# A hybrid encoder block: x2 read back behind the last sum's split, and the plain features' activations scaled by VectorE and made later

## The chip, the cores and the metric

The kernel runs on one core of one Trainium2 chip, as one program. The metric is the device time of an execution in microseconds (us). The time of the kernel before is the median of three runs, 719.93 us (717.46, 719.93 and 720.59).

## The reference

One layer of a streaming encoder on x of 512 tokens by 1024 channels, everything in float32. A first half (gated linear attention beside forgetting attention, merged by gates) gives the residual stream x2. The change lies in the second half, the gated MLP with a causal convolution of width 3 on its activation branch, and the final norm:

```python
    x = x + y @ w_out

    a, val = jnp.split(rmsnorm(x, norm_ffn_g) @ w_up, 2, axis=-1)
    a = causal_dwconv(a, conv_w, conv_b)
    return x + (jax.nn.gelu(a) * val) @ w_down
...
    return rmsnorm(x, norm_final_g)
```

`w_up` has 2 x 2816 columns (22 tiles of 128 features in each half), `w_down` 2816 rows.

## The kernel before, in words

**Splits.** Every product of matrices is made of three matmuls on halves in a reduced format (`mm3`, L248 to L250): high times high, low times high, high times low. So each piece of weights (128 x 1024 values) is loaded, cast by ScalarE to its high half (L217) and subtracted by VectorE to its low half (L218), into one of three pairs of buffers (`wh`, `wl`). `piece()` hands the pieces out in one fixed order and splits up to three ahead; a piece's buffers come free when TensorE is through with it.

**The up projection.** The first two feature tiles (`plain`) are made by plain products into four PSUM banks, for each tile one bank of activations `pa` and one of values `pv`. The other 20 tiles come in ten groups of two, by a scheme for 2 x 2 blocks with seven products instead of eight. Each group g has seven steps (g, p) with p from 1 to 7, and the steps of neighbouring groups are interleaved by a table (`SLOT`). A step is 24 matmuls of 256 columns. The operands of the seven products on the side of x are blocks of the normalised x2, or sums of them, kept as high and low halves (`xops`, made by `split_x`, L974 to L979). The tile `xo` holds those of products 1, 5 and 3. The weights of products 6, 7 and 4 are sums: the raw piece of an earlier step stays in its buffer, and when it has been split, a DMA on POOL's queue adds the next block to it in place (L225, `rawx<-in_wu_dram`). For a group that chain is 5 to 6 to 4, so the last sum of all is that of step (9, 4).

After step 6 and step 7 of a group, VectorE writes the activations before the convolution to the tile `ap` (L982, called from L1135 and L1137); `convolve` makes three taps (ScalarE at L1030, VectorE at L1034 twice) and the GELU (ScalarE, L1039) in the tile `t0`, of which there is one. After step 4, VectorE multiplies by the values (L1149) and makes sums for the down projection (`sums_of_acts`), which is done by seven products too. Its first pieces are multiplied already within the last group (`first_down`, after steps (9, 6) and (9, 7)).

**The plain features.** `plain_activations` (L1055) is called ahead of the fourth step (number 3 in the list of steps). For each of the two tiles: VectorE scales `pa` by the token's norm factor `rb` into `ap` (L1007 and L1059), `convolve` follows, POOL multiplies the GELU by `rb` in place (L1061), and VectorE multiplies that by `pv` from PSUM (L1062). At its end stand the sums and the first split of the two features (L1046, L1025, L1026). The table `ahead_of` (L1070) says what is called ahead of which step.

**x2's way back.** The first half writes x2 token by token to DRAM (`x2d`). It is read back into the place of `xo`, once the last product on `xo` is done, by a DMA on POOL's queue (L1162, 2 MB), together with the gain of the final norm, broadcast to all partitions (L1163). The first to read it are the additions of the down projection's products (`add`, L1227).

**Order.** Each engine runs its instructions in one fixed order, and DMAs are issued in the order of the queue of the engine that issues them (SyncE, POOL, ScalarE). The order is not simply that of the source: a planner runs the program dry with its own costs, takes among the instructions that are ready the one that is traced first or due first, and keeps that order. `tc.issue_after(i)` adds an edge, so that an instruction stands behind `i` on its engine.

Of the kernel before, what the change touches and what calls it, by code (L numbers as in the profile page):

```python
# [9 lines left out]
F32 = mybir.dt.float32  # L10
# [4 lines left out]
ALU = mybir.AluOpType  # L15
# [3 lines left out]
P = 128  # L19
T = 512  # L20
NT = T // P
D = 1024
# [28 lines left out]
NCL = 2  # L51
NSS = (NF - NCL) // 2
# [14 lines left out]
def hybrid_kernel(ctx: ExitStack, tc, xT, wp, wu, wd, wf, pp, aw2, qkg, fing, out):  # L67
    nc = tc.nc
# [33 lines left out]
    wsum = [dpool.tile([P, KB * 512], F32, name=f"wsum{i}") for i in range(4)]  # L102
# [19 lines left out]
    at_step = {}  # L122
# [50 lines left out]
    raws, splits, taken, first_copy, added, last_load = {}, [], [0], [], [], []  # L173
# [25 lines left out]
    def split_next():  # L199
        n = len(splits)  # L200
        if n not in raws:
            load_raw(n)
        raw, m = raws[n], recipes[n][2]
        if n in spare:
            hi, lo = spare[n]()
        else:
            hi = wpool.tile([P, 1024], F32R, tag="wh", name="wh", bufs=NW)
            lo = wpool.tile([P, 1024], F32R, tag="wl", name="wl", bufs=NW)
        if n < KD:
            if n > 0:  # L210
                nc.scalar.copy(out=hi[:, :WF], in_=raw)
            else:
                first_copy.append(nc.vector.tensor_copy(out=hi[:, :WF], in_=raw))  # L213
            nc.vector.tensor_sub(out=lo[:, :512], in0=raw[:, :512], in1=hi[:, :512].bitcast(F32))  # L214
            nc.vector.tensor_sub(out=hi[:, WF : WF + 64], in0=raw[:, 512:WF], in1=hi[:, 512:WF].bitcast(F32))
        else:
            nc.scalar.copy(out=hi[:, :m], in_=raw[:, :m])  # L217
            nc.vector.tensor_sub(out=lo[:, :m], in0=raw[:, :m], in1=hi[:, :m].bitcast(F32))  # L218
        splits.append((hi, lo))
        for what, i, *other in then.get(n, ()):  # L220
            if what == "load":
                load_raw(i)
            elif what == "add":
                raws[i] = raw
                added[:] = [nc.gpsimd.dma_start(raw, recipes[i][0], accum_op=ALU.add)]  # L225
            else:
                first_sum(i, *other, after=added[0])
        for i, b, c in sums_at.get(n, ()):
            if n < ADD_AT[0]:
                continue  # L230
            now = nc.gpsimd.tensor_copy(out=tick, in_=lo[:, 0:1].bitcast(F32))
            with tc.issue_after(now.ins):
                nc.gpsimd.dma_start(wsum[i][:, c], b[:, c], accum_op=ALU.add)

    def piece():
        n = taken[0]
# [70 lines left out]
    tick = cpool.tile([P, 1], F32, name="tick")  # L307
# [6 lines left out]
    def col(c, rows=P):  # L314
# [6 lines left out]
        out=negm, in_=negm, pattern=[[-1, P]], base=0, channel_multiplier=1, compare_op=ALU.is_ge, fill=-1e30  # L321
# [5 lines left out]
        out=gmask, in_=gmask, pattern=[[1, P]], base=0, channel_multiplier=-1, compare_op=ALU.is_ge, fill=0.0  # L327
# [5 lines left out]
    rb = cpool.tile([P, T], F32, name="rb")  # L333
# [79 lines left out]
    for k in range(KD):  # L413
        nc.scalar.activation(out=xh[k], in_=xrs[k], func=AF.Copy, scale=col(C_MIX + k))  # L414
        split_next()
        with tc.issue_after(first_copy[0].ins):
            nc.vector.scalar_tensor_tensor(
                out=xl[k], in0=xrs[k], scalar=col(C_MIX + k), in1=xh[k].bitcast(F32),
# [60 lines left out]
    for j in range(2):  # L479
# [4 lines left out]
            out=mz[:, j, :], in0=pz, scalar1=col(C_AB + j), scalar2=0.0, op0=ALU.add, op1=ALU.min  # L484
# [456 lines left out]
    for g in range(2):  # L941
        n = at_step[g, 5]
# [31 lines left out]
    def split_x(p, src, after=None):  # L974
        with tc.issue_after(after[0].ins) if after else ExitStack():
            hi = nc.scalar.copy(out=xops[p][0], in_=src)
        with tc.issue_after(after[1].ins) if after else ExitStack():
            lo = nc.vector.tensor_sub(out=xops[p][1], in0=src, in1=xops[p][0].bitcast(F32))
        return hi, lo  # L979
# [61 lines left out]
    def halves(x):  # L1041
        return x.rearrange("p (i t) -> p i t", t=H)

    def sums_of_acts(j, k):
        if j == 0:
            nc.vector.tensor_sub(out=s3[:, k], in0=a11[:, k], in1=a21[:, k])  # L1046
            split_act(0, a11, k)
        else:
            nc.vector.tensor_sub(out=s1[:, k], in0=a22[:, k], in1=a21[:, k])
            minus_sum(s2[:, k], s1[:, k], a11[:, k])  # L1050
            minus_sum(s4[:, k], a12[:, k], s2[:, k])

    last_gelu = None

    def plain_activations():  # L1055
        t0 = npool.tile([P, 2, T], F32, tag="t0", name="t0")
        for f, (pa, pv) in enumerate(plain):
            if f > 0:
                nc.vector.tensor_mul(out=ap[:, f, 2 : T + 2], in0=pa, in1=rb)  # L1059
            convolve(f, f, t0)  # L1060
            nc.gpsimd.tensor_mul(out=t0[:, f], in0=t0[:, f], in1=rb)  # L1061
            nc.vector.tensor_mul(out=act[0][:, :, f], in0=halves(pv), in1=halves(t0[:, f]))  # L1062
        sums_of_acts(0, slice(0, NCL))

    def p7_operand():
        nc.vector.tensor_sub(out=y3, in0=x11, in1=x21)
# [1 line left out]


    ahead_of = {  # L1070
        1: lambda: split_x(2, x12, third), 2: lambda: split_x(6, y2, third), 3: plain_activations, 4: p7_operand,
        5: lambda: split_x(4, x22, third),
    }

    def up_product(ps, p, first):
# [41 lines left out]

    st_of = {}
    for n, (g, p) in enumerate(steps):
        if n in ahead_of:  # L1120
            ahead_of[n]()
        st = st_of.setdefault(g, {})
        f = NCL + 2 * g
        name = {1: "x", 2: "x", 5: "z", 3: "z", 6: "y", 7: "y", 4: "y"}[p]
        first = name not in st
        if first:

            st[name] = (pax if name == "x" or g == 0 and name == "y" else pmm)()
        ps = st[name]
        up_product(ps, p, first)  # L1130
        if p in (1, 5, 3):
            st[p] = joint(ps)
        elif p == 6:
            nc.vector.tensor_add(out=ps, in0=ps, in1=st[1])
            minus_sum(ap[:, :, 2 : H + 2], halves(ps), halves(st[3]))  # L1135
        elif p == 7:
            minus_sum(ap[:, :, H + 2 : T + 2], halves(ps), halves(st[5]))  # L1137
            t0 = st["t0"] = npool.tile([P, 2, T], F32, tag="t0", name="t0")
            for i in range(2):
                convolve(f + i, i, t0)  # L1140
        elif p == 4:
            t0 = st["t0"]
            if f // KB == (f + 1) // KB:
                parts = [(f // KB, slice(f % KB, f % KB + 2), slice(0, 2))]
            else:
                parts = [((f + i) // KB, slice((f + i) % KB, (f + i) % KB + 1), slice(i, i + 1)) for i in range(2)]
            for i, c in enumerate((st["x"], ps)):
                for j, k, fs in parts:
                    nc.vector.tensor_mul(  # L1149
                        out=act[j][:, i, k], in0=halves(c)[:, fs], in1=t0[:, fs, i * H : (i + 1) * H]  # L1150
                    )
            for j, k, _ in parts:
                sums_of_acts(j, k)
        if g == NSS - 1 and p in EARLY:
            first_down(EARLY.index(p))
# [3 lines left out]
    xo2 = npool.tile([P, 6 * KH * H], F32, tag="xo", name="xo2")  # L1159
    x2t = xo2[:, : NT * D].rearrange("p (t d) -> p t d", d=D)  # L1160
    fgt = xo2[:, NT * D : (NT + 1) * D]
    nc.gpsimd.dma_start(x2t, x2d)  # L1162
    nc.gpsimd.dma_start(fgt, fing.broadcast_to([P, D]))  # L1163


    def in_place_of(tag, size):
# [210 lines left out]
```

## Time and profile before

| | us |
|---|---|
| median of three runs | 719.93 |
| profiled execution, its time | 717.68 |
| profiled execution, its span | 716.0 |
| TensorE busy | 703.1 (98%) |
| VectorE busy | 535.7 (75%) |
| ScalarE busy | 406.9 (57%) |
| POOL busy | 214.4 (30%) |
| mean granted clock of TensorE | 0.997 |

The profile is of one execution. Its span runs from the first to the last instruction; the execution's own time is 1.7 us longer. PE is TensorE, DVE VectorE, ACT ScalarE, POOL GpSimd, SP SyncE. A row of a timeline has start and duration in us, engine, line, operation, output and inputs, shape and count; in brackets stands how long the engine sat idle before it, and what ended that. A row of waits has who waited for whom, the us in total, the times, and the longest. The line of an operation is often that of a helper, such as `mm3`. [...] A row "DMA to landing" gives least, median and greatest time from issue to landing for the loads of one line.

The plain products end at 398.2 us, the steps run from there to 609.8 us, and the down projection to the end.

### The profile page before, as it was taken

Reading aid. Unit: us, or ns where it says so; the run is one execution under the profiler, and the core shown is the slowest. Engines: PE = TensorE matmul, PEld = TensorE weight load, DVE = VectorE, ACT = ScalarE, POOL = GpSimd, SP = SyncE. Lnnn points to the kernel's source line nnn. Section 1 sums busy time; section 2 is a strip of 40 time slices with the busy share of each in tenths; the row PEclk is TensorE's granted clock in tenths of the full one; section 3 lists DMA queues with packets and bytes.
Section 4 is the critical chain, followed back from the end, with each engine's and each line's share of the span. In section 5 each row is a group of like instructions: output and inputs, shape, how many; then the busy total and the mean of one; then the engine's idle time right before and its main releaser. Section 6 shows DMA issues by size and latency. Waiting matters only on the chain.

```text
span 716.0 us, 11179 instructions
## 1 busy us (share of the span) xinstructions
PE 703.1 (98%) x4186; PEld 612.9 (86%) x4186; DVE 535.7 (75%) x781; ACT 406.9 (57%) x646; POOL 214.4 (30%) x246
## 2 busy tenths in 40 slices
PE   8999999999999999999999999999999999999996
PEld 5887788888888888888788989999999998888885
DVE  7874596677866675566447988889888888997894
ACT  6484324588877742234553755565566565655663
POOL 7204333336342412223221252243434310000122
PEclk9999999999999999999999999999999999999998
DMA  8367745667568576766528488777777888576643
GB/s 282 123 237 199 257 142 198 221 153 181 152 135 202 120 194 159 171 166 163 176 89 253 115 177 191 171 180 180 184 174 192 203 188 298 165 220 202 178 147 118
DMA packets 45654, 129.87 MB, mean 181 GB/s; under 512 B 5000, under 2 KB 12312, under 8 KB 45472
## 3 DMA queue, kind: packets, MB, share of 16 engines
q1 hardware_dynamic: 31008, 92.91, 38.8%
q0 software_dynamic: 8352, 30.94, 24.9%
q10 hardware_dynamic: 6240, 5.31, 2.3%
q8 instruction: 33, 0.54, 0.3%
q14 instruction: 21, 0.17, 0.1%
HBM read 124.93 MB, written 27.28 MB: 213 GB/s over the span
## 4 chain that ended last, share of the span: by engine, by line
PE 87%; DVE 6%; ACT 3%; DMA 2%; issue 1%; SPq 0%; DVEq 0%; ACTq 0%
PE ps_mm L248 21%; PE ps_mm L249 21%; PE ps_mm L250 21%; PE ps_ax L250 6%; PE ps_ax L248 6%; PE ps_ax L249 6%; DVE wl L218 2%; DMA rawx<-in_wu_dram 1%; PE ps_pt L786 1%; ACT wh L217 1%; PE ps_po L810 1%; PE ps_ax L927 1%; DMA qf<-in_wf_dram 1%; DVE xs L1000 1%; PE ps_lg L760 1%
## 5 line engine op out<-in xcount | busy, mean ns | idle before, releaser
L248 PE MATMUL ps_mm<-xh,wh 128*128 128x512 f32 (+1 forms) x312 | 107.3, 345 | 1.0 <-DVE wh L213 1.0
L250 PE MATMUL ps_mm<-xh,wl 128*128 128x512 f32 (+1 forms) x312 | 106.5, 342 | 0.0
L249 PE MATMUL ps_mm<-xl,wh 128*128 128x512 f32 (+1 forms) x312 | 106.2, 341 | 0.0
L217 ACT CAST wh<-rawx 128x1024 fp32r<-128x1024 f32 x75 | 76.2, 1015 | 52.3 <-PE ps_mm L249 22.6
L218 DVE TENSOR_TENSOR wl<-rawx,wh 128x1024 fp32r<-128x1024 f32 x75 | 88.7, 1190 | 16.6 <-ACT wh L217 16.5
L217 ACT CAST wh<-raw 128x1024 fp32r<-128x1024 f32 x61 | 63.9, 1049 | 56.7 <-PE ps_mm L249 41.8
L218 DVE TENSOR_TENSOR wl<-raw,wh 128x1024 fp32r<-128x1024 f32 x61 | 84.0, 1377 | 10.4 <-ACT wh L217 7.4
L248 PEld LDWEIGHTS ps_mm<-xh,wh 128*128 128x128 f32 x312 | 59.1, 190 | 7.8 <-ACT xh L414 1.9
L250 PEld LDWEIGHTS ps_mm<-xh,wl 128*128 128x128 f32 x312 | 59.1, 190 | 7.6 <-DVE wl L214 0.5
L217 ACT CAST wh<-rawz 128x1024 fp32r<-128x1024 f32 x28 | 29.3, 1047 | 61.9 <-PE ps_mm L249 29.8
L249 PEld LDWEIGHTS ps_mm<-xl,wh 128*128 128x128 f32 x312 | 59.3, 190 | 5.9
L225 POOL DMA_DIRECT2D rawx<-in_wu_dram x30 | 26.1, 869 | 102.3 <-DVE wl L218 94.9
L248 PE MATMUL ps_mm<-wh,xh 128*128 128x512 f32 x140 | 55.4, 397 | 0.1
L249 PE MATMUL ps_mm<-wl,xh 128*128 128x512 f32 x140 | 54.7, 391 | 0.0
L250 PE MATMUL ps_mm<-wh,xl 128*128 128x512 f32 x140 | 54.6, 390 | 0.0
L218 DVE TENSOR_TENSOR wl<-rawz,wh 128x1024 fp32r<-128x1024 f32 x28 | 40.2, 1435 | 8.2 <-ACT wh L217 8.1
L191 POOL TENSOR_TENSOR rawx<-rawx,raw 128x256 f32<-128x256 f32 x32 | 38.2, 1222 | 25.4 <-DMA rawx<-in_wu_dram 25.4
L248 PE MATMUL ps_mm<-xo,wh 128*128 128x256 f32 x160 | 45.4, 284 | 0.0
L250 PE MATMUL ps_mm<-xo,wl 128*128 128x256 f32 x160 | 45.3, 283 | 0.0
L249 PE MATMUL ps_mm<-xo,wh 128*128 128x256 f32 x160 | 45.3, 283 | 0.0
L248 PE MATMUL ps_mm<-xc,wh 128*128 128x256 f32 (+1 forms) x128 | 42.6, 333 | 1.5 <-DVE ap L982 1.5
L1034 DVE SCALAR_TENSOR_TENSOR t<-ap,ppt,t 128x512 f32<-128x512 f32 x44 | 43.9, 1051 | 0.0
(385 smaller groups left out, 1973.9 us busy)
## 6 DMA issues: line engine op xcount, KB each, us to landing
rawx<-in_wu_dram POOLq DMA_DIRECT2D x32, 512.0 KB, 6.7
rawz<-in_wp_dram SPq DMA_DIRECT2D x28, 512.0 KB, 4.3
raw<-in_wp_dram SPq DMA_DIRECT2D x28, 512.0 KB, 4.3
wsum<-in_wd_dram SPq DMA_DIRECT2D x20, 512.0 KB, 6.6
raw<-in_wu_dram SPq DMA_DIRECT2D x20, 512.0 KB, 4.8
rawx<-in_wu_dram SPq DMA_DIRECT2D x20, 512.0 KB, 6.2
rawx<-wsum SPq DMA_DIRECT2D x12, 512.0 KB, 4.1
wsum<-in_wd_dram POOLq DMA_DIRECT2D x10, 512.0 KB, 8.0
```

The lines of the kernel that those rows point to most:

```text
L191: nc.gpsimd.tensor_add(out=raws[n][:, c], in0=raws[n][:, c], in1=raws[other][:, c])
L217: nc.scalar.copy(out=hi[:, :m], in_=raw[:, :m])
L218: nc.vector.tensor_sub(out=lo[:, :m], in0=raw[:, :m], in1=hi[:, :m].bitcast(F32))
L225: added[:] = [nc.gpsimd.dma_start(raw, recipes[i][0], accum_op=ALU.add)]
L248: mm(ps, lhsT=ah, rhs=bh, start=start, stop=False, **k)
L249: mm(ps, lhsT=ah, rhs=bl, start=False, stop=False, **k)
L250: mm(ps, lhsT=al, rhs=bh, start=False, stop=stop, **k)
L760: mm(lg[:, :n], lhsT=qt0[:, q], rhs=kt[:, :n], start=True, stop=False)
L786: nc.tensor.transpose(pt[:, c], pr[:, c], ident)
L810: mm(po[h][:, q], lhsT=w, rhs=pl[:, kb, lo:], start=False, stop=(kb == nk - 1))
L927: nc.tensor.transpose(pt[:, tt * P : (tt + 1) * P], xr[:, tt * P : (tt + 1) * P], ident)
L1034: nc.vector.scalar_tensor_tensor(out=t0[:, i], in0=ap[:, i, w : w + T], scalar=col(C_CW + w * NF + f), in1=t0[:, i], op0=ALU.mult, op1=ALU ...
```

## The change

Two parts.

First, the issue of x2's way back. The copy-and-issue pair that the first half uses for its own sums (a POOL copy of one column of a split's low half into `tick`, and the DMA edged behind that copy) becomes a function, `dma_behind`. The two loads of L1162 and L1163 go through it, with the low half of the split of step (9, 4), the last sum. So they are issued when that split is done.

Second, the plain features. `plain_activations` is taken apart: `plain_gelus` (scaling into `ap`, convolution, GELU) stays ahead of step 3. POOL's product with `rb` goes; instead VectorE multiplies `pv` by `rb` in place in PSUM (`plain_values`), ahead of step 2 for the first tile and of step 7 for the second. The product of the two (`plain_act`) comes ahead of step 4 and step 7, the sums and the split of the two features ahead of step 10, and the split of x's block for product 4 moves from ahead of step 5 to ahead of step 6.

```diff
         for i, b, c in sums_at.get(n, ()):
             if n < ADD_AT[0]:
                 continue
-            now = nc.gpsimd.tensor_copy(out=tick, in_=lo[:, 0:1].bitcast(F32))
-            with tc.issue_after(now.ins):
-                nc.gpsimd.dma_start(wsum[i][:, c], b[:, c], accum_op=ALU.add)
+            dma_behind(lo, wsum[i][:, c], b[:, c], accum_op=ALU.add)
+
+    def dma_behind(lo, out, in_, **k):
+
+        now = nc.gpsimd.tensor_copy(out=tick, in_=lo[:, 0:1].bitcast(F32))
+        with tc.issue_after(now.ins):
+            return nc.gpsimd.dma_start(out, in_, **k)
...
-    def plain_activations():
+    plain_t0 = []
+
+    def plain_gelus():
         t0 = npool.tile([P, 2, T], F32, tag="t0", name="t0")
+        plain_t0.append(t0)
         for f, (pa, pv) in enumerate(plain):
             if f > 0:
                 nc.vector.tensor_mul(out=ap[:, f, 2 : T + 2], in0=pa, in1=rb)
             convolve(f, f, t0)
-            nc.gpsimd.tensor_mul(out=t0[:, f], in0=t0[:, f], in1=rb)
-            nc.vector.tensor_mul(out=act[0][:, :, f], in0=halves(pv), in1=halves(t0[:, f]))
-        sums_of_acts(0, slice(0, NCL))
+
+    def plain_values(f):
+        pv = plain[f][1]
+        nc.vector.tensor_mul(out=pv, in0=pv, in1=rb)
+
+    def plain_act(f):
+        nc.vector.tensor_mul(out=act[0][:, :, f], in0=halves(plain[f][1]), in1=halves(plain_t0[0][:, f]))
...
     ahead_of = {
-        1: lambda: split_x(2, x12, third), 2: lambda: split_x(6, y2, third), 3: plain_activations, 4: p7_operand,
-        5: lambda: split_x(4, x22, third),
+        1: (lambda: split_x(2, x12, third),), 2: (lambda: split_x(6, y2, third), lambda: plain_values(0)),
+        3: (plain_gelus,), 4: (p7_operand, lambda: plain_act(0)), 6: (lambda: split_x(4, x22, third),),
+        7: (lambda: plain_values(1), lambda: plain_act(1)), 10: (lambda: sums_of_acts(0, slice(0, NCL)),),
     }
...
-        if n in ahead_of:
-            ahead_of[n]()
+        for what in ahead_of.get(n, ()):
+            what()
...
-    nc.gpsimd.dma_start(x2t, x2d)
-    nc.gpsimd.dma_start(fgt, fing.broadcast_to([P, D]))
+
+    last_lo = splits[at_step[NSS - 1, 4]][1]
+    dma_behind(last_lo, x2t, x2d)
+    dma_behind(last_lo, fgt, fing.broadcast_to([P, D]))
```

## The prediction

> **What bounds the kernel now.** I read the busy times on the page first, then the list of waits of TensorE over the whole span, and then each long wait back to its cause with the chain of waits and the engines' timelines.
>
> ```profile
> PE 703.1 (98%) x4186; PEld 612.9 (86%) x4186; DVE 535.7 (75%) x781; ACT 406.9 (57%) x646; POOL 214.4 (30%) x246
> PE ps_ax L250 <- DVE wl L218: 2.0, 2, 1.7
> PE ps_mm L248 <- DVE ap L982: 1.5, 1, 1.5
> ```
>
> TensorE is busy for 98% of the span of 716.0 us, so little gets shorter here except by taking away time in which it stands still. Two rows of its waits lie in the steps: 2.0 us (two waits) for a split of weights by VectorE, and 1.5 us for `ap` by VectorE. These 3.5 us, 0.49% of the span, are what this change can address; no part of it removes a matmul.
>
> The three waits, on TensorE's timeline:
>
> ```profile
> 404.66 0.39 PE L250 MATMUL ps_ax<-xh,wl 128*128 128x256 f32 x1 [0.34 <-DVE wl L218]
> ...
> 419.30 0.28 PE L249 MATMUL ps_ax<-xl,wh 128*128 128x256 f32 x1
> 421.23 0.39 PE L250 MATMUL ps_ax<-xh,wl 128*128 128x256 f32 x1 [1.66 <-DVE wl L218]
> ...
> 602.94 0.28 PE L250 MATMUL ps_mm<-xh,wl 128*128 128x256 f32 x1
> ...
> 604.90 0.39 PE L250 MATMUL ps_ax<-wh,actl 128*128 128x512 f32 x1
> 606.81 0.36 PE L248 MATMUL ps_mm<-xc,wh 128*128 128x256 f32 x1 [1.52 <-DVE ap L982]
> ```
>
> The first matmul behind a wait lasts 0.36 to 0.39 us, one in the stream 0.28. So each wait that goes gives about 0.1 us more than its own length.
>
> **Part A: x2's way back.** The chain of waits around the last of them:
>
> ```profile
> 592.35 10.44 DMA rawx<-in_wu_dram
> 602.88 1.06 ACT wh L217
> ...
> 606.07 0.61 DVE ap L982
> 606.81 0.36 PE ps_mm L248
> ```
>
> The load that adds the last sum (block 4 of group 9, issued at 592.35) takes 10.44 us to land. Its cast and its split follow, and because VectorE works in order, `ap` of step 7, whose product was done at 603.2 (602.94 + 0.28), stands behind that split; step 4's product needs `ap`'s bank. POOL's timeline shows what went ahead of the load on the same queue, and the listing of the POOL loads' line gives their usual time:
>
> ```profile
> 588.60 0.56 POOL L1162 DMA_DIRECT2D xo<-x2d  x1 [5.24 <-PE ps_mm L250]
> 592.35 0.86 POOL L225 DMA_DIRECT2D rawx<-in_wu_dram  x1 [3.19 <-DVE act L1149]
> DMA to landing us min/median/max: 5.5/6.7/10.4
> xo<-x2d POOLq DMA_DIRECT2D x1, 2048.0 KB, 10.4
> ```
>
> x2 (2 MB) is on its way from 588.60 to 599.0. The load behind it is the slowest of its 30 (maximum 10.4, median 6.7). The change puts both x2 and the gain row behind a small POOL copy that reads the low half of that very split. The load itself still goes at about 592.35, since a VectorE row releases it, not x2. With the median it lands at 599.05. The way from landing to TensorE was 606.81 - 602.79 = 4.02 us, which gives 603.1; but `ap` also needs step 7's product, so about 603.2 + 0.7 + 0.14 = 604.0. TensorE is busy until 605.29 (604.90 + 0.39). The wait of 1.52 goes whole, with 1.3 us in hand, and it stays gone as long as the load takes under 605.29 - 4.02 - 592.35 = 8.9 us. Term A: 1.52 + 0.1 = 1.6 us; bounds 0 (the load keeps its 10.4) and 1.6. A loss would need x2 to take over 15 us on its new way (below), half as long again as its own row.
>
> What A adds: one copy of a column and a wait on POOL. Behind it in POOL's order stand only x2, the gain row and, much later, the residual's products. x2 now starts at about 602.5 (split done at 602.2, the copy 0.2). With its old 10.4 us it lands at 613. These rows are the copy's line, a tail load on SyncE's queue, that load's cast, the first addition to x2, and the time to landing of SyncE's loads from 560 us on:
>
> ```profile
> L231 POOL COPY tick<-wl x24: 179/186/516, 140.6 to 329.7; 128x1 f32<-128x1 f32 x24
> 605.22 0.33 SPq L185 DMA_DIRECT2D rawx<-in_wd_dram  x1
> 613.01 0.61 ACT L217 CAST wh<-rawx 128x512 fp32r<-128x512 f32 x1
> 619.18 0.68 DVE L1227 TENSOR_TENSOR xo<-xo,ps_ax 128x512 f32<-128x512 f32 x1
> DMA to landing us min/median/max: 2.6/4.3/8.9
> ```
>
> Its first reader is the addition that began at 619.18; 1.6 us earlier that is 617.6, 4.6 us after the landing. The gain row is read only in the residual. So A adds nothing to the path: cover is 4.6 us, and each microsecond beyond it would stall VectorE.
>
> [...] The tail load issued at 605.22 would leave 3.0 us earlier (the split that frees its buffer ended at 605.2 and now ends at 602.2) and is cast at 613.01, so by these rows it has 7.8 us now, and keeps about 9 where TensorE gains 1.6. [...]
>
> **Part B: the plain features.** VectorE's timeline ahead of the long wait:
>
> ```profile
> 403.38 1.22 DVE L218 TENSOR_TENSOR wl<-raw,wh 128x1024 fp32r<-128x1024 f32 x1
> ...
> 408.07 0.69 DVE L1062 TENSOR_TENSOR act<-ps_mm,t 128x512 f32<-128x512 f32 x1 [1.20 <-POOL t L1061]
> ...
> 415.82 0.69 DVE L1062 TENSOR_TENSOR act<-ps_mm,t 128x512 f32<-128x512 f32 x1 [1.19 <-POOL t L1061]
> 416.43 0.69 DVE L1134 TENSOR_TENSOR ps_ax<-ps_ax,joint 128x512 f32<-128x512 f32 x1
> 417.03 0.68 DVE L1046 TENSOR_TENSOR s<-act 128x512 f32<-128x512 f32 x1
> 417.62 0.69 DVE L1026 TENSOR_TENSOR actl<-act,acth 128x512 fp32r<-128x512 f32 x1
> 418.23 0.69 DVE L982 SCALAR_TENSOR_TENSOR ap<-ps_ax,joint 128x512 f32<-128x512 f32 x1
> 418.83 1.22 DVE L978 TENSOR_TENSOR xc<-xs,xc 128x1024 fp32r<-128x1024 f32 x1
> 419.96 3.49 DVE L218 TENSOR_TENSOR wl<-rawx,wh 128x1024 fp32r<-128x1024 f32 x3
> ```
>
> VectorE has no other pause between 403 and 422. The split of block 7 (419.96, done 421.2) is what TensorE wanted at 419.42. Step by step ahead of it:
> - Removed: the two pauses for POOL's products, 1.20 + 1.19 = 2.39 us.
> - Added: two in-place products in PSUM. The same form stands in the rows (`ps_ax<-ps_ax,joint`, 0.69 us, the next one 0.60 later): 2 x 0.60 = 1.2 us.
> - Moved to later steps: the second feature's product (0.61), the difference (0.59), the split of the two features (0.61), and the split of x's block 4 (1.13), together 2.9 us. None issues a DMA, and POOL's queue only gets shorter.
>
> So the split of block 7 starts 2.39 - 1.2 + 2.9 = 4.1 us earlier, at 415.9, ends at 417.1 and has 2.3 us in hand. If the planner left all moved work ahead of it, it would start 1.2 us earlier and 0.56 us of the wait would stay. The gain is 1.66 + 0.1, at the low end 1.1.
>
> On the other side stands the wait of 0.34 at 404.66. The first new product needs only a finished bank, so the planner can fill it into an earlier pause of its own model; VectorE's real timeline has none, and the split at 403.38 would come 0.60 later: -0.6 us. If it is put behind (where its step stands), 0. I take -0.2, nearer to 0, since the rows show VectorE with no pause there that the planner could fill. Term B: 1.75 - 0.2 = 1.5, bounds 0.5 and 1.75.
>
> What is late next is the split for step 6 of each group:
>
> ```profile
> 426.71 4.17 DVE L1034 SCALAR_TENSOR_TENSOR t<-ap,ppt,t 128x512 f32<-128x512 f32 x4
> 430.82 1.21 DVE L218 TENSOR_TENSOR wl<-rawx,wh 128x1024 fp32r<-128x1024 f32 x1
> 432.85 0.28 PE L250 MATMUL ps_mm<-xh,wl 128*128 128x256 f32 x1
> ```
>
> It ends at 432.03, 0.8 us ahead of its use. The moved 2.9 us and the last product must fit in ahead of 422; the 2.3 us in hand and the pauses that VectorE takes for TensorE's pace hold them, and then the shift passes through unchanged.
>
> **Sum.** A 1.6 + B 1.5 = 3.1 us. The profiled execution took 717.68 us outside its span of 716.0, so it would take 714.6 (span 712.9). The median of the runs shown is 719.93, 2.25 above it, and two of the four executions lie at each level. Their mean is 718.9; I carry the gain to that: 718.9 - 3.1 = 715.8 us.
>
> **Rivals.**
> 1. One of the two waits stays, or another takes its place: the load of the last sum still takes over 8.9 us, or the product filled in ahead costs 0.6 and part of the moved work stays ahead. For it: VectorE works back to back through this stretch but for the two pauses. Against: both causes are named by rows. Gain 1.5 us: 717.4.
> 2. Nothing moves: the load's 10.4 us come from SyncE's loads and not from x2, and the planner keeps VectorE's order. For it: SyncE's loads in that stretch were also slow, up to 8.9 against a median of 4.3. Against: they were slow while x2 ran. Then 718.9.
> 3. Slower: the planner's dry run decides VectorE's order from its own times, which the edit changes. The place is step 6 of groups 1 to 9, with its 0.8 us in hand. One moved split (1.13) and one product (0.60) ahead of it would cost 1.73 - 0.8 = 0.93 us a group, 8.4 over nine, against the 3.1 gained: 718.9 + 5.3 = 724.2. It decides from 0.8 + 3.1/9 = 1.1 us of additional work per group. Against: only the first group's work moves.
>
> **How the numbers follow.** The sum 0.57, rival 1 0.23, rival 2 0.08, rival 3 0.12. A change of 0.5%, 3.6 us, is about what a measurement of this kernel can tell. The sum lies just below it: its upper bound is 1.6 + 1.75 = 3.35, and the unseen share of the waits could add a little, so I give it 0.36 of its 0.57 for faster, and 0.02 of rival 1. That makes faster 0.38, same 0.50, slower 0.12. The range: low, the sum's upper bound from the profiled level less the scatter downwards (717.5 - 3.35 - 1.6 = 712.5); high 720.5, which takes in rivals 1 and 2 at the upper level and leaves out most of rival 3.
>
> **What would show it.** Right: no wait of TensorE for `ap` L982 near 605; the last POOL load of `rawx` landing in about 7 us and x2's issue behind it; no VectorE pause for POOL near 408 and 416; TensorE's waits for L218 down from 2.0 to under 1 us. Wrong: a first addition to x2 that waits for a DMA, a wait above 0.8 at the second step, or new waits once a group. The prediction is wrong if both waits go and the time still falls by less than 1.5 us, or if it rises.

## The result, and the profile after

The changed kernel took 715.58 us (median of 8 executions, 714.64 to 716.76), the kernel before on the same chip 720.02 us (8, 717.46 to 722.82): a ratio of 0.9942, 95% interval 0.9923 to 0.9961. The profiled execution took 714.64 us with a span of 712.9 us. The forecast was 715.8 us, and 712.9 us for the span.

The page after, its busy times, and the one row of TensorE's waits that lies in the steps:

```profile
PE 702.7 (99%) x4186; PEld 613.2 (86%) x4186; DVE 537.4 (75%) x783; ACT 406.6 (57%) x646; POOL 207.6 (29%) x246
```

```profile
PE ps_ax L254 <- DVE wl L218: 0.7, 2, 0.4
```

VectorE does 1.7 us more and POOL 6.8 us less; neither decides. The waits of TensorE in the steps fell from 3.5 to 0.7 us, and the row for `ap` is gone. (The lines moved by four or so: `mm3` is now L252 to L254.) TensorE's timeline after, at the first step, at its two waits, at the first piece of the down projection, and where the wait for `ap` was:

```profile
397.98 0.28 PE L252 MATMUL ps_ax<-xo,wh 128*128 128x256 f32 x1
...
404.40 0.39 PE L254 MATMUL ps_ax<-xh,wl 128*128 128x256 f32 x1 [0.28 <-DVE wl L218]
...
413.99 0.39 PE L254 MATMUL ps_ax<-xo,wl 128*128 128x256 f32 x1 [0.43 <-DVE wl L218]
...
595.28 0.40 PE L252 MATMUL ps_ax<-wh,acth 128*128 128x512 f32 x1
...
603.41 0.39 PE L254 MATMUL ps_ax<-wh,actl 128*128 128x512 f32 x1
603.64 0.28 PE L252 MATMUL ps_mm<-xc,wh 128*128 128x256 f32 x1
```

Step (9, 4) starts at 603.64 right behind the piece before it, without a wait: 0.23 us after the start of that piece's last matmul, whose row has 0.39 us (such rows overlap). The wait of 1.66 for block 7 is gone too; a new one, 0.43, stands at the step (1, 1).

The same three marks in the kernel before:

```profile
398.17 0.28 PE L248 MATMUL ps_ax<-xo,wh 128*128 128x256 f32 x1
...
596.77 0.40 PE L248 MATMUL ps_ax<-wh,acth 128*128 128x512 f32 x1
```

and 606.81 for (9, 4). They cut the span in four: up to the first step; from there to the first piece of the down projection (part B lies here); from there to step (9, 4) (part A); from there to the end. Before: 398.17, 198.60, 10.04, 109.19. After: 397.98, 197.30, 8.36, 109.26. So B gave 1.30 us and A 1.68 us, and these two are the difference of the spans but for 0.1.

POOL's timeline after, with x2's new way:

```profile
590.23 0.85 POOL L225 DMA_DIRECT2D rawx<-in_wu_dram  x1 [8.36 <-DVE wl L218]
601.20 0.18 POOL L235 COPY tick<-wl 128x1 f32<-128x1 f32 x1 [10.13 <-DVE wl L218]
602.33 0.57 POOL L237 DMA_DIRECT2D xo<-x2d  x1 [0.95 <-PE ps_mm L254]
602.90 0.20 POOL L235 COPY tick<-wl 128x1 f32<-128x1 f32 x1
603.02 0.54 POOL L237 DMA_DIRECT2D xo<-in_fing_dram  x1
```

The listing of the POOL loads' line (L225) and the list of DMA issues give the times to landing after:

```profile
DMA to landing us min/median/max: 5.4/6.5/8.2
```

```profile
xo<-x2d POOLq DMA_DIRECT2D x1, 2048.0 KB, 9.1
```

The last sum's load no longer takes 10.4 us; no load of that line takes over 8.2. x2 is issued at 602.33 and is there 9.1 us later, at 611.4. The last sum's load itself left 192.25 us after the first step, and not 194.18 as before. B's 1.30 us is in that; the 0.6 us besides had not been forecast ("still goes at about 592.35"), and why it left earlier was not followed up.

VectorE's timeline after, from the plain features and from the first addition to x2:

```profile
395.59 0.69 DVE L1071 TENSOR_TENSOR ps_mm<-ps_mm,rb 128x512 f32<-128x512 f32 x1
...
403.13 1.22 DVE L218 TENSOR_TENSOR wl<-raw,wh 128x1024 fp32r<-128x1024 f32 x1
...
406.72 1.23 DVE L218 TENSOR_TENSOR wl<-rawx,wh 128x1024 fp32r<-128x1024 f32 x1 [1.23 <-ACT wh L217]
...
411.58 1.21 DVE L982 TENSOR_TENSOR xc<-xs,xc 128x1024 fp32r<-128x1024 f32 x1
412.72 1.22 DVE L218 TENSOR_TENSOR wl<-raw,wh 128x1024 fp32r<-128x1024 f32 x1
...
416.72 1.21 DVE L218 TENSOR_TENSOR wl<-rawx,wh 128x1024 fp32r<-128x1024 f32 x1
...
615.76 0.68 DVE L1241 TENSOR_TENSOR xo<-xo,ps_ax 128x512 f32<-128x512 f32 x1
```

The pauses for POOL are gone; one of 1.23 us for a cast has come at 406.72. The split of block 7 starts at 416.72, not 419.96. The split of x's block 4 (`xc`, 411.58), which the edit moves to a later step, stands earlier than before (418.83), and directly ahead of the split at 412.72 that TensorE then waits 0.43 us for. The first addition to x2, at 615.76, waits for nothing, 4.3 us after the landing.

### The profile page after: what moved, and what is told of

Same layout as the page of the kernel before. It is cut to its first block, busy times and chain, and to the rows that moved or that the text cites. A ratio compares the mean times of both kernels' runs of the same rounds, so it can differ in the third digit from the quotient of the medians.

```text
span 712.9 us, 11181 instructions
## 1 busy us (share of the span) xinstructions
PE 702.7 (99%) x4186; PEld 613.2 (86%) x4186; DVE 537.4 (75%) x783; ACT 406.6 (57%) x646; POOL 207.6 (29%) x246
## 4 chain that ended last, share of the span: by engine, by line
PE 84%; DVE 6%; DMA 3%; ACT 3%; issue 2%; POOL 1%; SPq 0%; DVEq 0%; ACTq 0%; POOLq 0%
PE ps_mm L252 20%; PE ps_mm L254 20%; PE ps_mm L253 20%; PE ps_ax L254 6%; PE ps_ax L253 6%; PE ps_ax L252 6%; DMA cb<-nct 2%; DVE wl L218 2%; ACT wh L217 1%; PE ps_pt L790 1%; DMA wsum<-in_wd_dram 1%; PE ps_ax L931 1%; DVE xs L1004 1%; DMA qf<-in_wf_dram 1%; PE ps_po L814 1%
## 5 line engine op out<-in xcount | busy, mean ns | idle before, releaser
L252 PE MATMUL ps_mm<-xh,wh 128*128 128x512 f32 (+1 forms) x312 | 107.3, 345 | 1.1 <-DVE wh L213 1.1
L254 PE MATMUL ps_mm<-xh,wl 128*128 128x512 f32 (+1 forms) x312 | 106.4, 342 | 0.0
L252 PEld LDWEIGHTS ps_mm<-xh,wh 128*128 128x128 f32 x312 | 59.2, 190 | 7.7 <-ACT xh L418 1.8
L254 PEld LDWEIGHTS ps_mm<-xh,wl 128*128 128x128 f32 x312 | 59.1, 190 | 7.4 <-DVE wl L214 0.4
L225 POOL DMA_DIRECT2D rawx<-in_wu_dram x30 | 25.7, 856 | 113.2 <-DVE wl L218 106.0
L252 PE MATMUL ps_mm<-wh,xh 128*128 128x512 f32 x140 | 55.4, 397 | 0.1
L254 PE MATMUL ps_mm<-wh,xl 128*128 128x512 f32 x140 | 54.6, 390 | 0.0
L252 PE MATMUL ps_mm<-xo,wh 128*128 128x256 f32 x160 | 45.4, 284 | 0.0
L254 PE MATMUL ps_mm<-xo,wl 128*128 128x256 f32 x160 | 45.3, 283 | 0.0
L252 PE MATMUL ps_mm<-xc,wh 128*128 128x256 f32 (+1 forms) x128 | 42.5, 332 | 0.0
```

The costliest lines, as they stand in the source:

```text
L252: mm(ps, lhsT=ah, rhs=bh, start=start, stop=False, **k)
L254: mm(ps, lhsT=al, rhs=bh, start=False, stop=stop, **k)
```

## The experiments

Medians are in us; the ratio is to the kernel before on the same chip. The four stages are those defined above, read off TensorE's timeline in each kernel's profiled execution; the first, ahead of the change, varies by up to 2.3 us between executions of whatever kernel (in one profile 1.25 us lie at the start, as the last section shows), so the stages tell more than the spans. The last column is the time to landing of the last sum's load, or, marked <, the longest of its line.

| kernel | median (executions) | ratio, 95% interval | first step | to first piece (B) | to (9, 4) (A) | to the end | landing |
|---|---|---|---|---|---|---|---|
| before | 720.02 (8) | 1 | 398.17 | 198.60 | 10.04 | 109.19 | 10.4 |
| after | 715.58 (8) | 0.9942 (0.9923-0.9961) | 397.98 | 197.30 | 8.36 | 109.26 | < 8.2 |
| a_only | 715.61 (5) | 0.9954 (0.9937-0.9970) | 397.93 | 198.60 | 8.37 | 109.00 | < 8.7 |
| b_only | 718.00 (12) | 0.9980 (0.9966-0.9995) | 397.99 | 197.41 | 10.89 | 109.41 | 11.3 |
| b_vec_only | 718.61 (10) | 0.9984 (0.9971-0.9996) | 397.66 | 197.64 | 10.41 | 110.69 | 10.8 |
| b_late_only | 718.49 (10) | 0.9980 (0.9965-0.9996) | 399.57 | 196.65 | 10.65 | 110.53 | 11.0 |
| before_again | 718.79 (10) | 0.9996 (0.9979-1.0013) | 397.80 | 198.62 | 10.68 | 110.70 | 11.1 |
| x2_on_sync | 717.66 (10) | 0.9978 (0.9962-0.9995) | 399.64 | 198.60 | 9.58 | 109.98 | 10.6 |
| x2_more | 723.37 (8) | 1.0049 (1.0029-1.0068) | 397.79 | 198.61 | 12.60 | 110.50 | 13.6 |
| x2_later | 717.99 (10) | 0.9980 (0.9962-0.9998) | 399.30 | 197.44 | 8.37 | 110.99 | < 8.9 |
| tied0 | 714.54 (6) | 0.9939 (0.9921-0.9957) | 399.95 | 196.66 | 8.36 | 109.03 | < 8.0 |
| a_late | 714.51 (5) | 0.9926 (0.9907-0.9945) | 397.82 | 196.67 | 8.37 | 109.04 | < 8.3 |

**a_only: x2 alone behind the split.** The plain features stay as they were.

```diff
-    nc.gpsimd.dma_start(x2t, x2d)
-    nc.gpsimd.dma_start(fgt, fing.broadcast_to([P, D]))
+    last_lo = splits[at_step[NSS - 1, 4]][1]
+    dma_behind(last_lo, x2t, x2d)
+    dma_behind(last_lo, fgt, fing.broadcast_to([P, D]))
```

> Part A alone: x2 and the gain row behind the split of the last sum, the plain features as before. My theory (x2 held up the load of the last sum): the load issued near 592.3 lands in 5.5 to 8.9 us instead of 10.4, TensorE's wait of 1.5 us for ap is gone, the two waits of the plain features (0.34 and 1.66) stay; span about 714.2, 1.8 less than before. If the time of that load also differs from execution to execution in the kernel before, the median gains more than that (2 to 3 us) and the runs scatter less than before (5.4 us from lowest to highest). Rival (the load is slow whatever x2 does): the wait for ap stays above 1 us and the span within 0.5 of 716.0.

Its list of waits of TensorE has one row in the steps:

```profile
PE ps_ax L254 <- DVE wl L218: 2.0, 2, 1.7
```

The wait for `ap` is gone and the two for splits of weights stand as before; the A stage is 8.37 as in the full change, the B stage 198.60 as before. A alone moves the median by 4.1 us (0.46%), more than the 2 to 3 us expected and more than its stage's 1.67 us (0.23% of 718) explains. The last section comes back to the rest.

**b_only: the plain features alone.** x2 goes back as before.

```diff
-    last_lo = splits[at_step[NSS - 1, 4]][1]
-    dma_behind(last_lo, x2t, x2d)
-    dma_behind(last_lo, fgt, fing.broadcast_to([P, D]))
+    nc.gpsimd.dma_start(x2t, x2d)
+    nc.gpsimd.dma_start(fgt, fing.broadcast_to([P, D]))
```

(against the changed kernel)

> Part B alone: the plain features as in the changed kernel, x2 loaded as before. Theory: the wait of 1.66 us goes, a wait of about 0.4 us at step (1, 1) comes instead, and the wait for ap near 604 stays at 1 to 2 us; span about 714.7, 1.3 less than before. The scatter of the runs stays that of the kernel before, if it comes from the load of the last sum. Rival (the two parts only work together): the span falls by less than 0.5.

Its waits:

```profile
PE ps_mm L252 <- DVE ap L986: 2.4, 1, 2.4
PE ps_ax L254 <- DVE wl L218: 0.8, 2, 0.5
```

The B stage is 197.41, 1.19 us shorter, and the wait for `ap` stays, with 2.35 us longer than the 1 to 2 expected. The parts are independent: each one's stage is that of the full change to about 0.1 us, with or without the other.

**b_vec_only and b_late_only: the two halves of B.** The first keeps the old places of all calls and only lets VectorE scale in PSUM; the second keeps POOL's product and only moves the calls to later steps. Both leave x2 as before.

```diff
+    def plain_all():
+        plain_gelus()
+        for f in range(2):
+            plain_values(f)
+            plain_act(f)
+        sums_of_acts(0, slice(0, NCL))
...
-        1: (lambda: split_x(2, x12, third),), 2: (lambda: split_x(6, y2, third), lambda: plain_values(0)),
-        3: (plain_gelus,), 4: (p7_operand, lambda: plain_act(0)), 6: (lambda: split_x(4, x22, third),),
-        7: (lambda: plain_values(1), lambda: plain_act(1)), 10: (lambda: sums_of_acts(0, slice(0, NCL)),),
+        1: (lambda: split_x(2, x12, third),), 2: (lambda: split_x(6, y2, third),), 3: (plain_all,),
+        4: (p7_operand,), 5: (lambda: split_x(4, x22, third),),
```

```diff
     def plain_values(f):
-        pv = plain[f][1]
-        nc.vector.tensor_mul(out=pv, in0=pv, in1=rb)
+        t0 = plain_t0[0]
+        nc.gpsimd.tensor_mul(out=t0[:, f], in0=t0[:, f], in1=rb)
...
-        1: (lambda: split_x(2, x12, third),), 2: (lambda: split_x(6, y2, third), lambda: plain_values(0)),
-        3: (plain_gelus,), 4: (p7_operand, lambda: plain_act(0)), 6: (lambda: split_x(4, x22, third),),
+        1: (lambda: split_x(2, x12, third),), 2: (lambda: split_x(6, y2, third),),
+        3: (plain_gelus, lambda: plain_values(0)), 4: (p7_operand, lambda: plain_act(0)),
+        6: (lambda: split_x(4, x22, third),),
```

(both against the changed kernel; the lines that put x2 back are those of b_only)

> Only VectorE's scaling in PSUM in place of POOL's product; all calls ahead of the steps where they were before, x2 as before. Theory (the pauses that VectorE made for POOL caused the long wait): the two pauses of 1.2 us are gone, the split for step (0, 7) starts near 418.4 instead of 419.96, and the wait there falls from 1.66 to 0.2 to 0.5 us; span 714.6 to 715.0. Rival (the moved work was the cause, not POOL): the wait stays above 1.2 us, since VectorE has two products more to do.

> Only the later places: POOL's product with the norm factor stays (called after the GELUs for the first tile, ahead of step 7 for the second), VectorE has no scaling in PSUM, x2 as before. Theory (either half is enough, because what counts is how much stands ahead of one split): a pause of about 1.2 us for POOL stays ahead of the first product, none ahead of the split for step (0, 7), which starts near 417 and causes no wait; span 714.3 to 714.8. Rival (only taking POOL out helps): the wait at step (0, 7) stays above 1 us.

Their rows of waits for splits, first b_vec_only:

```profile
PE ps_ax L254 <- DVE wl L218: 0.9, 2, 0.6
```

and b_late_only:

```profile
PE ps_ax L254 <- DVE wl L218: 0.3, 1, 0.3
```

Scaling on VectorE gives 0.96 us of the B stage (198.60 to 197.64), and 0.56 us of the wait for block 7 stays. The later places give 1.95 us, more than both halves together (1.30), and leave only the old wait of 0.3. So the gain of B is in where the work stands. The medians of these two do not show that: both have the wait for `ap` (1.89 and 2.13 us) and a last stage 1.3 to 1.5 us longer, and so their spans, 716.4 and 717.4 us, missed the 714.3 to 715.0 expected.

**before_again: the kernel before, unchanged** (its diff is empty), for the scatter of its profile.

> The kernel before once more, with a second profile. Theory of the scatter (the time of the last sum's load, 10.4 us in the first profile, differs from execution to execution): it lands in another time, 9 to 13 us, and the wait for ap moves by the same amount. Rival: the same 10.4 and 1.5 us to 0.2, and the span differs elsewhere if at all.

The times agree (0.9996), but the profiled execution differs from the first one of before. TensorE's timeline:

```profile
607.10 0.35 PE L248 MATMUL ps_mm<-xc,wh 128*128 128x256 f32 x1 [2.16 <-DVE ap L982]
...
608.31 0.41 PE L248 MATMUL ps_mm<-xc,wh 128*128 128x256 f32 x1
608.52 0.41 PE L249 MATMUL ps_mm<-xc,wh 128*128 128x256 f32 x1
...
611.29 0.41 PE L250 MATMUL ps_mm<-xc,wl 128*128 128x256 f32 x1
```

and its windows (busy time of PE, PEld, DVE, ACT, POOL with counts, then the granted clock, the DMA engines' busy share and GB/s):

```profile
606.00:608.00 2.00, 0.90 (x7) 0.93 (x8) 2.00 (x3) 1.01 (x2) 0.00 (x0) 1.00 0.49 131
608.00:610.00 2.00, 2.00 (x12) 2.00 (x11) 2.00 (x5) 1.97 (x3) 0.00 (x0) 0.54 0.46 68
610.00:612.00 2.00, 2.00 (x12) 1.92 (x11) 1.88 (x3) 1.05 (x2) 0.00 (x0) 0.61 0.49 195
```

The wait is 2.16 us, not 1.52, and the load took 11.08 us, not 10.44: both are longer by 0.64 us. From 1.2 us after the wait, matmuls follow each other at 0.21 us instead of 0.12, and the granted clock is 0.54 and 0.61. Step (9, 4) takes 4.41 us (607.10 to 611.51) instead of 2.95, and the last stage is 1.5 us longer.

**x2_on_sync: the kernel before with x2 issued by SyncE.**

```diff
-    nc.gpsimd.dma_start(x2t, x2d)
-    nc.gpsimd.dma_start(fgt, fing.broadcast_to([P, D]))
+    nc.sync.dma_start(x2t, x2d)
+    nc.sync.dma_start(fgt, fing.broadcast_to([P, D]))
```

> The kernel before with x2 and the gain row issued from SyncE's queue instead of POOL's, at about the same moment (588 us), so the same bytes are on the way beside the load of the last sum, but not ahead of it on its own queue. If it is the order on one queue: the load lands in 5.5 to 8 us, the wait for ap falls below 0.3 us, span 714.0 to 714.5. If it is the bytes on the shared DMA engines: the load still takes 9 to 11 us and the wait for ap stays at 1 to 1.6 us, span near 716.

x2's issue on SyncE's timeline, the load in the chain of waits, and TensorE's wait:

```profile
589.80 0.33 SPq L1162 DMA_DIRECT2D xo<-x2d  x1
```

```profile
593.20 10.60 DMA rawx<-in_wu_dram
```

```profile
607.82 0.36 PE L248 MATMUL ps_mm<-xc,wh 128*128 128x256 f32 x1 [1.05 <-DVE ap L982]
```

With nothing of x2 on POOL's queue the load takes 10.60 us, as long as before. So it is slow not because it stands behind x2 in a queue, but because both move at once: with x2 issued behind the split (a_only) no load of its line takes over 8.7. The wait is 0.5 us shorter because the load starts earlier, 193.6 us after the first step instead of 194.2. (The last stage, 0.8 us longer than in the first profile of before, was not followed up.) The windows of the kernel before show the DMA engines full while the load is on its way:

```profile
600.00:602.00 2.00, 2.00 (x18) 1.91 (x17) 1.50 (x3) 0.11 (x1) 0.00 (x0) 1.00 1.04 344
602.00:604.00 2.00, 2.00 (x16) 1.83 (x15) 0.03 (x1) 1.12 (x2) 0.00 (x0) 1.00 1.02 416
604.00:606.00 2.00, 1.29 (x6) 0.75 (x4) 2.00 (x3) 1.62 (x2) 0.00 (x0) 1.00 0.56 227
```

(The DMA share is 0.91 to 1.09 in every window of 2 us from 592 to 604, with the landing at 602.8, and 0.56 in the next.)

**x2_more: the kernel before with 1 MB more on the way.** A copy in DRAM that nobody reads is issued just ahead of x2; the orders of the engines are otherwise those of before. (`dma_behind` is the function of the change.)

```diff
+    x2e = dpool.tile([P, NT, D], F32, name="x2e")
...
-    nc.gpsimd.dma_start(x2t, x2d)
+
+    early = splits[at_step[NSS - 1, 2]][1]
+    ahead = dma_behind(early, x2e[:, :2], x2d[:, :2])
+    with tc.issue_after(ahead.ins):
+        nc.gpsimd.dma_start(x2t, x2d)
```

> The kernel before, with 1 MB of additional transfer: behind the split for step (9, 2), just ahead of x2 on POOL's queue, half of x2's array is copied in DRAM to a second array that nobody reads. No engine's order changes but for POOL's copy and that issue. If the load of the last sum is slow because of the bytes that are on the way at the same time, 1 MB more (x2's 2 MB took 10.4 us) makes it land about 5 us later, 15 to 16 us from issue, and the wait for `ap` grows from 1.5-2.2 to 6-7 us; the median rises by about 5 us to 724-726. If its slowness were its own (the accumulation, SyncE's loads), 10 to 11.3 us and a wait of 1.5 to 2.4 stay, median 719-720. It is also a wait that is surely long: if a wait of about 2 us can lower the clock, this one should show a granted clock of about 0.5 for some 3.4 us soon after it, and a step (9, 4) of about 4.4 us instead of 2.9; if the low clock of three executions had another cause, step (9, 4) may stay at 2.9.

The load in the chain of waits, the row of waits, and one window:

```profile
591.36 13.62 DMA rawx<-in_wu_dram
```

```profile
PE ps_mm L252 <- DVE ap L987: 4.1, 1, 4.1
```

```profile
610.00:612.00 2.00, 2.00 (x12) 2.00 (x11) 2.00 (x4) 1.86 (x3) 0.00 (x0) 0.50 0.47 92
```

The load takes 13.6 us, 2.5 to 3.2 more than the profiles of before, and the wait is 4.07 us: the direction of the account by bytes, at 50 to 64% of the size expected of it (5 us); the median, 723.37, is below the 724 to 726 expected for the same reason. Part of the added megabyte had passed by then: the copy was issued at 587.91 and is listed with 6.9 us to its landing, so only the last 3.4 us of it fall into the load's time. And the clock falls again: 0.50 in the window behind the wait, step (9, 4) 4.43 us, the last stage 110.50.

**x2_later: the change, with x2 issued behind a later split**, that of the last early piece of the down projection.

```diff
-    last_lo = splits[at_step[NSS - 1, 4]][1]
-    dma_behind(last_lo, x2t, x2d)
-    dma_behind(last_lo, fgt, fing.broadcast_to([P, D]))
...
+    later = splits[at_last[NPB - 1]][1]
+    dma_behind(later, x2t, x2d)
+    dma_behind(later, fgt, fing.broadcast_to([P, D]))
```

> The changed kernel with x2 and the gain row later still, behind the split of the last piece of the first product of the down projection (near 611 instead of 602 us). My cover of 4.6 us says: x2 lands near 620, its first reader wants it near 616, VectorE stands still for about 4.5 us with splits behind it, and TensorE then waits 1 to 4 us; span 714 to 717. Rival (the additions have more room than that, since the banks that they read are not needed soon): no wait of TensorE, span within 0.4 of the changed kernel's.

The chain of waits, VectorE's and TensorE's timelines:

```profile
613.76 8.98 DMA xo<-x2d
```

```profile
622.76 3.68 DVE L1238 TENSOR_TENSOR xo<-xo,ps_ax 128x512 f32<-128x512 f32 x6 [1.64 <-DMA xo<-x2d]
```

```profile
627.63 0.50 PE L253 MATMUL ps_mm<-wl,xh 128*128 128x512 f32 x1 [1.33 <-DVE wl L218]
```

Issued at 613.76 instead of 602.33, x2 lands at 622.7, VectorE stands 1.64 us for it and then makes up six additions in a row, and TensorE waits 1.33 us for the split behind them. The last stage is 1.7 us longer, the A stage the same 8.37. So the cover of x2's new place has an end. VectorE was expected to stand for about 4.5 us; it stood for less because the planner changed its order: in the change the first addition (615.76) comes ahead of the split at 616.36, and here two splits and three other instructions come ahead of all additions. So this run does not measure the size of the cover.

**tied0: the change, with the first product in PSUM held behind the split of x for product 6**, so that the planner cannot fill it in ahead.

```diff
+    sixth = []
...
-        nc.vector.tensor_mul(out=pv, in0=pv, in1=rb)
+        with tc.issue_after(sixth[0][1].ins):
+            nc.vector.tensor_mul(out=pv, in0=pv, in1=rb)
...
-        1: (lambda: split_x(2, x12, third),), 2: (lambda: split_x(6, y2, third), lambda: plain_values(0)),
+        1: (lambda: split_x(2, x12, third),), 2: (lambda: sixth.append(split_x(6, y2, third)), lambda: plain_values(0)),
```

> The changed kernel with one edge more: the first product in PSUM stands behind the low half of the split for product 6. In the order that the planner makes of it the split of x's block 4 also falls back behind ap of step (0, 6). Theory (what was filled in ahead makes the wait of 0.43 us at step (1, 1)): that wait goes, the one of 0.28 at the second step stays at 0.2 to 0.4, span 712.3 to 712.6, in the time no more than 0.1% less than the changed kernel. Rival: the wait at (1, 1) comes from the load of a sum that lands late and stays.

Its waits in the steps are down to one:

```profile
PE ps_ax L254 <- DVE wl L218: 0.3, 1, 0.3
```

The B stage is 196.66, 0.64 us shorter than in the change. The new wait of 0.43 is gone: with that product elsewhere the planner puts the split of x's block 4 behind the split for (1, 1). The one that stays is the old 0.34 at the second step, so the product filled in ahead was not what it hung on. (The span, 714.0 us for the 712.3 to 712.6 expected, is longer by its first stage, 399.95.)

**a_late: part A, and of part B only the later places.** POOL still multiplies the GELU; this is b_late_only with the change's way for x2.

```diff
-    nc.gpsimd.dma_start(x2t, x2d)
-    nc.gpsimd.dma_start(fgt, fing.broadcast_to([P, D]))
+    last_lo = splits[at_step[NSS - 1, 4]][1]
+    dma_behind(last_lo, x2t, x2d)
+    dma_behind(last_lo, fgt, fing.broadcast_to([P, D]))
```

(against b_late_only)

> Part A as in the change; of part B only the later places: POOL still multiplies the GELU by the norm factor, and no product in PSUM is added. My theory (the later places alone clear the wait for the split of block 7; VectorE's scaling in PSUM only saves pauses that nobody then waits for): TensorE waits in the steps only 0.3 us for the second step's split, none for `ap`; stage up to the first down-projection piece 196.6 to 196.7 us, the next stage 8.4; median 714 to 715, ratio to before about 0.994, no worse than the change itself. Rival (without the scaling in PSUM, a pause of VectorE for POOL, 1.2 us, comes back in front of some split): a wait of 0.5 to 1.2 us for a split among the first ten steps, median 715.5 to 716.5.

A VectorE row and the row of TensorE's waits:

```profile
407.73 0.69 DVE L1074 TENSOR_TENSOR act<-ps_mm,t 128x512 f32<-128x512 f32 x1 [1.20 <-POOL t L1071]
```

```profile
PE ps_ax L254 <- DVE wl L218: 0.3, 1, 0.3
```

VectorE's pause of 1.20 us for POOL is back, and no wait of TensorE follows from it. The stages are those of tied0 (196.67 and 8.37), the medians the same (714.51 and 714.54). The scaling in PSUM, 1.2 us of work for VectorE, isn't needed once the calls stand later. Both kernels are about 1 us faster than the change, which is at the edge of what these runs tell: the executions of a_late (713.62 to 714.73) and the change (714.64 to 716.76) hardly overlap, but they ran beside different runs of before, and the intervals of the ratios do.

## Why the prediction held, step by step

**Part A, 1.6 us: measured 1.68.** The wait for `ap` went whole, as worked out, and so did the cost of the first matmul behind it: step (9, 4) takes 2.87 us instead of 2.95. The load landed within the 8.9 us that the working allowed (no load of the line took over 8.2). x2 was issued at 602.33 (602.5 forecast) and landed after 9.1 us; the cover at the first addition was 4.3 us (4.6 forecast). x2_later took that cover away and paid for it, though in another order of VectorE's work.

One step of A failed in its cause: "what went ahead of the load on the same queue". x2_on_sync shows that the queue is not what makes the load slow: 10.60 us with x2 on SyncE's queue, 10.44 on POOL's. x2_more shows that the bytes on the way beside it do: 13.62 with 1 MB more. The size came out right because in either account the change takes x2 out of the load's time. A reader of the wrong cause would have tried another queue, and gained 0.22% (interval 0.05 to 0.38) instead of the 0.46% (0.30 to 0.63) of a_only.

SyncE's loads for the down projection, beside which x2 moves now, took no longer than before. Their listing from 560 us on, after:

```profile
DMA to landing us min/median/max: 2.7/4.3/8.4
```

It was 2.6/4.3/8.9 before.

**Part B, 1.5 us: measured 1.30.** The wait for block 7, 1.66, went whole. Its split starts at 416.72; 415.9 had been worked out, and the pause of 1.23 at 406.72 for a cast, which the working did not have, is more than the difference. The planner did fill the first product in ahead (395.59), as feared, but something else made room: the split at 403.13 comes no later, and the second step's wait is 0.28 instead of 0.34, not 0.94. So the 0.2 taken off there was not paid. What was paid is the new wait of 0.43 at step (1, 1), and this is the step that failed: "What is late next is the split for step 6 of each group". The search for the next late split began behind the wait that goes; the one that became late stands ahead of it, because the planner put work that was moved to a later step earlier. tied0 shows the price: 0.64 us. The waits once a group did not come.

**The working's view of B's cause** was half right. It put 4.1 us of room down to 1.2 us net from POOL's pauses and 2.9 us from the later places. b_vec_only shows the first alone as not enough (0.56 us of the wait stays, which is the figure that the working gave for it), b_late_only and a_late the second alone as enough.

**The sum.** 3.1 us was forecast and the span fell by 3.1 us; A's +0.1 and B's -0.2 are made up by 0.19 ahead of the first step, which is scatter. The carried time, 715.8, is 0.2 us above the median, and that closeness is partly luck. The prediction took the two levels among the four executions of before as mere scatter and carried the gain to their mean, 718.9. The median of eight is 720.02, 1.1 us more, and the medians differ by 4.4 us, 1.3 more than the 3.1 forecast; the two misses cancel. The 3.1 us still lie in the interval of the ratio (0.39 to 0.77%, or 2.8 to 5.5 us). The working left out one thing that the runs show: in the profile of before_again the granted clock is at 0.54 and 0.61 in the windows behind the wait that A removes, and the last stage is 1.5 us longer.

**The rivals.** Rival 1 came true in kind only: another wait took a place, with 0.43 us instead of the 1.5 us priced. Rival 2, that the 10.4 us come from SyncE's loads, falls with a_only: moving x2 alone makes the wait go. Rival 3, more work ahead of step 6 in each group, did not happen.

## What to carry to other kernels

Here a load of 512 KB took 10.4 to 11.3 us beside a transfer of 2 MB, on POOL's queue or on SyncE's, and at most 8.7 with that transfer issued behind it. So it pays to issue a large transfer that nobody needs soon behind the last small one that somebody waits for: look for the load with the longest time to landing and ask what else was moving. Where a planner orders the work, moving a call to a later step may move the instruction earlier; read the order that came out, ahead of the place of the edit as well. And before paying another engine to remove a pause, see whether anything waits for what stands behind that pause.

## What the runs showed of the hardware that was not expected

**The granted clock behind the wait for `ap`.** Seven profiles have this wait. Behind it the granted clock fell in four of them (to 0.50 in the windows of b_late_only and x2_more that the fall fills), where TensorE had waited 1.89 us (b_vec_only), 2.13 us (b_late_only), 2.16 us (before_again) and 4.07 us (x2_more). The windows of 2 us behind the wait lose 1.7 us of full clock in each of the four, which is 3.4 us at 0.50 (in before_again, by its 0.54 and 0.61, from about 608.2 to 611.6), and step (9, 4) took 4.41 to 4.45 us instead of 2.9. It did not fall after 1.05 (x2_on_sync), 1.52 (before) and, in b_only, 2.35 us. So the length of the wait alone does not decide.

Two windows behind the wait, first b_late_only, then b_only:

```profile
606.00:608.00 2.00, 1.13 (x8) 1.16 (x9) 2.00 (x4) 1.24 (x2) 0.00 (x0) 0.90 0.47 131
608.00:610.00 2.00, 2.00 (x11) 2.00 (x11) 2.00 (x4) 1.85 (x4) 0.00 (x0) 0.50 0.51 115
```

```profile
606.00:608.00 2.00, 1.71 (x14) 1.74 (x15) 2.00 (x4) 1.82 (x3) 0.00 (x0) 1.00 0.29 101
608.00:610.00 2.00, 2.00 (x16) 1.87 (x15) 2.00 (x4) 1.86 (x4) 0.00 (x0) 1.00 0.76 238
```

b_only, with the longer wait of the two, keeps 1.00, and its last stage is 109.41 us where that of b_late_only is 110.53. What does decide was not shown.

**What of this is in the times.** The 29 executions of the kernel before that ran beside before_again lie at 717.2 to 718.4 us (14) and 719.5 to 722.3 us (15), none between; the 29 beside a_only show 7 up to 718.7 and 22 from 719.1 on, so hardly a gap. The upper times are not all executions with the fall. Each execution's mean granted clock is on record. By the 3.4 us at 0.50 a fall should take 0.0024 of it (half of 3.4 us in 717, an estimate), and in the profiles it is 0.997 to 0.999 without the fall and 0.995 to 0.997 with it. Of the 37 upper executions 23 have at most 0.996, which no lower one has, and 11 have 0.999, which by this estimate leaves no room for a fall. The four kernels without a wait for `ap` and with x2 at its new place (after, a_only, tied0, a_late) have no execution below 0.997 among 24; x2_later, with the other wait that it has, has one at 0.995.

Another cause of a longer time lies at the start, where no part of the change reaches. Two matmuls in x2_on_sync, and the same two in the first profile of before:

```profile
9.08 0.63 PE L249 MATMUL ps_mm<-xl,wh 128*128 128x512 f32 x1
9.50 0.63 PE L250 MATMUL ps_mm<-xh,wl 128*128 128x512 f32 x1
```

```profile
8.02 0.39 PE L249 MATMUL ps_mm<-xl,wh 128*128 128x512 f32 x1
8.25 0.39 PE L250 MATMUL ps_mm<-xh,wl 128*128 128x512 f32 x1
```

They follow each other at 0.42 us in x2_on_sync and at 0.23 in before, and the second starts 1.25 us later. The first stage of x2_on_sync is 1.47 us longer (399.64 against 398.17). Why the matmuls are slower there was not shown.

So the rest of part A's gain in the median can only be estimated. The stage gives 1.67 us, from a profile with a wait of 1.52. The waits in the five profiles with x2 beside the load on POOL's queue (before, before_again, b_only, b_vec_only, b_late_only) are 2.0 us in the mean, 0.5 more. The fall, 1.5 us, taken to be in the 23 of these 58 executions with at most 0.996, gives 0.6 in the mean. Together that is 2.8 us of the 4.1 by which a_only's median is lower; the interval of its ratio reaches from 2.2 to 4.5 us.

**What the last sum's load took.** A load of that line (512 KB) takes 6.5 us in the median (after; 6.7 before), 10.4 to 11.3 us with x2's 2 MB moving beside it, and 13.6 us with a copy of 1 MB more, which overlapped it for 3.4 us.
